# The first output slab is loaded into the weight tiles of the last heads, and the plan's due times for the next slabs and for the new rows' scores are changed

## The chip, the cores and the metric

The kernel runs on one core of a Trainium2 chip. The core has a matrix engine (TensorE, PE in the profile), a vector engine (VectorE, DVE), a scalar engine (ScalarE, ACT), a general engine (GpSimd, POOL) and a queue engine (SyncE, SP). Every engine takes its instructions in order; semaphores join them. 16 transfer engines (DMA) carry data between the memory (HBM) and the core's own memory (SBUF); transfers are issued from SP's and from POOL's queue. TensorE writes its products into eight banks of a small memory (PSUM). The metric is the device time of one execution in microseconds.

## What is computed

The reference is one step of a two-layer decoder for a prompt of 512 rows and for 8 sequences with 4 new rows each (the sample), 1024 wide, with the same weights for both. Layer one has a pooling branch and an attention to 256 memory tokens. Layer two, whose end matters here, has multi-head attention over a shared latent: 8 heads, a latent of 256 and a rotary key of 64. The prompt attends to itself, causally; each sample sequence attends to 4096 cached rows, which lie in 32 pages of 128 rows, and to its own new rows. The heads' results and four memory heads, each times its gate, are 1536 columns; they go through one output projection `w_out` (1536 x 1024), are added to the stream, and a last RMS norm gives `y_prompt` and `y_sample`:

```
mixed = concat([tok * silu(gate_t), mem_o * silu(gate_m)], -1)     # 1536 wide
x = x + mixed @ w_out[l]
y = rmsnorm(x, g_final)
```

All is in 32-bit floats. To be exact on TensorE the prompt's operands are split into a high half (a rounded copy, written by ScalarE) and a low half (the remainder, written by VectorE), and each product is made from three: high x high, high x low, low x high.

## The kernel before

The part that matters is the second layer's attention and its output. There TensorE's order and SP's order are fixed by hand: the program text is their order. The text is written by a small planner, `weave` (line 999). It holds several generators, called threads. Each either yields a condition that must hold before it goes on, or yields the time on TensorE that it has just planned; the plan's clock `now[0]` then moves on by that much. Of the threads that may go on, the one with the smallest `behind()` comes next. Two counters, `act` and `dve`, reckon with the time of ScalarE and VectorE, and `banks` (line 997) notes until when each kind of PSUM bank is held; `tr` has one bank, `ac`, `pa` and `hs` have two each. The plan is a reckoning only: on the chip every instruction waits for its semaphores. ScalarE, VectorE and POOL are not ordered by hand; a scheduler orders them by what it reckons to be ready.

These threads matter. `round_scores` and `round_values` (lines 1069 and 1138) run through the cached pages in 16 rounds of 16 pages, half a round at a time: `turn_keys` transposes the key columns of two pages (`b`) into the bank `tr`, the scores follow; the values take the transposed softmax weights, and once they have read a page buffer, `load_half` puts the next pages' loads on SP's queue (line 1056). `weights_ahead` (line 1261) splits the heads' weights. It runs for the query weights and for four pairs of key and value weights, 8 loads `wu` of 256 KB from POOL's queue into two tiles; each load goes out once the split of two loads before has freed its tile. `scores` and `heads` make the eight prompt heads; a head's `turn_weights` transposes its softmax weights, and its values follow.

When the last head's scores are planned, the pool `heads_in` is closed, and `fin` takes its memory (line 1488): three raw tiles `wr` of 512 KB, three high halves `wh`, three low halves `wl`. The last stage then plans six threads together (line 1669). `own_scores` (line 1638) multiplies the new sample rows' queries with their own keys, 24 products into the bank `tr`, which VectorE reads (line 1652). `first_slabs` (line 1528) loads the first three slabs of `w_out` from POOL's queue and splits them; a slab is 256 rows of `w_out` by 512 columns, the unit in which the output projection runs, and the first three hold heads 0 and 1, 2 and 3, 4 and 5. `mix_b` splits the gated heads themselves. `out_all` runs the output projection of the prompt: first the three slabs for the first 128 rows, then all six for the rest.

Of the kernel before, what the change touches and what calls it, by code (L numbers as in the profile page):

```python
# [8 lines left out]
F32R = mybir.dt.float32r  # L9
# [6 lines left out]
P = 128  # L16
# [22 lines left out]
def trunk_kernel(ctx: ExitStack, tc: tile.TileContext, A, O):  # L39
    nc = tc.nc  # L40
# [35 lines left out]
    def fr(ap):  # L76
        return ap.bitcast(F32)
# [10 lines left out]
    def split(h, l, src, eng=None):  # L88
        nc.scalar.copy(h, src)  # L89
        (eng or nc.vector).tensor_tensor(out=l, in0=src, in1=fr(h), op=ALU.subtract)  # L90
        return h, l
# [51 lines left out]
    for k in range(KD):  # L143
        nc.sync.dma_start(xT[k], A["x_T"][k])
        if k in (0, 3):
            c = slice(k and 4, k + 4 + (k > 0))
# [69 lines left out]
    def load_w(src, k, c):  # L216
        t = pw("wr")
        v = t[:, : k * c].rearrange("p (k c) -> p k c", k=k)
        nc.sync.dma_start(v, src)
        return t, v  # L220

    def split_w(t, k, c, eng=None, pool=None):
        n = k * c
        pool = pool or pw
        h, l = split(pool("wh", F32R, n), pool("wl", F32R, n), t[:, :n], eng)
        return h.rearrange("p (k c) -> p k c", k=k), l.rearrange("p (k c) -> p k c", k=k)
# [293 lines left out]
    for k in range(KD):  # L520
        for i in range(2):
            wh, wl = (t.rearrange("p (k c) -> p k c", k=KD) for t in fw[i])
# [13 lines left out]
    t, v = load_w(wa[22], KD, P)  # L536
    wh, wl = split_w(t, KD, P)
# [133 lines left out]
    order = [8, 9, 10, 11, 6, 7, 4, 5, 2, 3, 0, 1]  # L671
# [3 lines left out]
    for f in range(KD):  # L675
        pts = [ps_("pa"), ps_("pa")]
        for s in range(2):
            t = pw("wr")
            nc.sync.dma_start(t[:, :768], wo[f, s].rearrange("p k c -> p (k c)"))
            wh, wl = split_w(t, 6, P, nc.gpsimd)  # L680
# [32 lines left out]
    for f in (2, 0, 1):  # L713
        c = P if f < 2 else 64
        t, v = load_w(wkv[:, f * P : f * P + c].rearrange("(k p) c -> p k c", p=P), KD, c)
        if f < 2:
            wh, wl = split_w(t, KD, c)
# [28 lines left out]
    for j in range(4):  # L746
        t = xo("o")
# [220 lines left out]
    now = [0.0]  # L968
# [13 lines left out]
    act, dve = Queue(), Queue()  # L982
# [14 lines left out]
    banks = {t: Slots(n) for t, n in (("tr", 1), ("ac", 2), ("pa", 2), ("po", 1), ("hs", 2))}  # L997
# [30 lines left out]
    def ps_(tag):  # L1028
        return (rb if tag in rb.tags else hb)(tag)

    def width(n, full):

        return 0.13 + (full - 0.13) * n / 512

    hq = Pool("hq", "right", qw=(384, 2), tab=(512, 2), wu=(512, 2))
# [209 lines left out]
    total = 122.0  # L1245
# [12 lines left out]
    def pat(tag, dt=F32, n=None):  # L1258
        return next(p for p in (hq, heads_val, heads_in) if tag in p.tags)(tag, dt, n)

    def weights_ahead(raw, load, total, tags, n_cols, at):

        for n in range(total):
            yield lambda: n < 2 or at[n - 2][0] is None
            yield lambda: act.free <= now[0] + 0.2 and dve.free <= now[0] + 0.4
            t = split(pat(tags[0], F32R), pat(tags[1], F32R), raw.pop(n))
            done = dve(act(now[0], width(n_cols, 0.6)), width(n_cols, 0.69))
            at[n] = [t, done]
            if n + 2 < total:
                raw[n + 2] = load(n + 2)  # L1270
            yield 0.0, 5.0 if n else 0.0

    q_at, pair_at = {}, {}

# [150 lines left out]
    def heads():  # L1425
# [49 lines left out]
    rope_x, rope_of, inputs_of, valued_by, es_of = {}, {}, {}, {}, {}  # L1475
    first = [
        Thread(weights_ahead(raw_q, load_q, 12, ("qh", "ql"), 384, q_at), -2.0, 0.0, 1.0, now[0]),
        Thread(weights_ahead(raw_pair, load_pair, 8, ("wuh", "wul"), 512, pair_at), -1.5, 0.0, 1.0, now[0]),
        Thread(ropes(), -1.0, 0.0, 1.0, now[0]),
    ]  # L1480
# [7 lines left out]
    fin = Pool("fin", "left", wr=(D, 3), wh=(D, 3), wl=(D, 3), lo=(512, 1))  # L1488
    mixed = {}

    def load_mix(k):
        if k in (6, 7) or k < 4:
            return gt[k][:, :SEQ]
        t = pat("tab")
        nc.gpsimd.dma_start(t, gmd[k - 8] if k >= 8 else ad[k - 4])
        return t

    def mix_b(k, t=None):
        t = load_mix(k) if t is None else t
        low = fin("lo", F32R) if k == 0 else pg("g", F32R) if k < 4 else pat("p", F32R) if k >= 8 else pt("t", F32R)  # L1500
        mixed[k] = split(pc("c", F32R), low[:, :SEQ], t)
# [2 lines left out]
    ssq = st(16)  # L1504
    sss = st(2)
    slabs = [(fh, s) for fh in range(2) for s in range(6)]
    order = ([0, 1], [2, 3], [4, 5], [8, 9], [10, 11], [6, 7])

    def slab(t, fh, s, queue=None):
        k = order[s][0]  # L1510
        v = t.rearrange("p (k c) -> p k c", k=2)
        src = wo[k * P : (k + 2) * P, fh * 512 : (fh + 1) * 512]
        (queue or nc.sync).dma_start(v, src.rearrange("(k p) c -> p k c", p=P))
        return v

    def prepare(fh, s, t=None):
        if t is None:
            if fh == 0:
                for k in order[s]:
                    mix_b(k)  # L1520
            t = fin("wr")
            slab(t, fh, s)
        wh, wl = split(fin("wh", F32R), fin("wl", F32R), t)
        return wh.rearrange("p (k c) -> p k c", k=2), wl.rearrange("p (k c) -> p k c", k=2)

    prepared, prepared_at = [], []

    def first_slabs():

        raw = [fin("wr") for s in range(3)]  # L1530
        for s, t in enumerate(raw):
            slab(t, *slabs.pop(0), nc.gpsimd)
        at = now[0] + 4.0
        for s in range(3):
            yield lambda: gt[order[s][1]] is not None
            mix = [(k, load_mix(k)) for k in order[s]]
            for k, t in mix:
                yield lambda: act.free <= now[0] + 0.2 and dve.free <= now[0] + 0.4
                mix_b(k, t)
                dve(act(now[0], 0.57), 0.69)  # L1540
            yield lambda: at + 2.0 * s <= now[0] and act.free <= now[0] + 0.2 and dve.free <= now[0] + 0.4
            prepared.append(prepare(0, s, raw[s]))
            prepared_at.append(dve(act(now[0], 1.04), 1.2))

# [17 lines left out]
    def out_rows(fh):  # L1562
# [50 lines left out]
        for s in range(6):  # L1613
            wh, wl = prepared.pop(0)
            late.append((s, wh, wl))
            if s == 4:
                continue
            for j in range(fh == 0 and s < 3, 4):
                for p, piece in enumerate(pieces[j]):
                    for one in late:  # L1620
                        run(one[0], j, piece, *one[1:])
                        yield 1.4 / len(pieces[j]), 0.0
                    if s == 5:
                        if not x1n:
                            yield lambda: x1n
                        done(j, p, *piece)
            for _ in late:
                if slabs:
                    prepared.append(prepare(*slabs.pop(0)))
            late = []  # L1630
# [6 lines left out]

    def own_scores():

        ps = ps_("tr")  # L1640
        sv = ps[:NS, :NS].rearrange("p (b t) -> p b t", b=NB)
        for b in range(NB):
            for k in range(2):
                nc.tensor.matmul(
                    sv[:, b, :], lhsT=QT[:, k, b, :], rhs=ckT_s[:, k, b * NT : (b + 1) * NT], start=k == 0, stop=False
                )
            nc.tensor.matmul(
                sv[:, b, :], lhsT=Qr[:, b, 0, :], rhs=krT_s[:, b * NT : (b + 1) * NT], start=False, stop=True
            )
        w = pat("qw")  # L1650
        tail = w[:NS, :NS].rearrange("p (b t) -> p b t", b=NB)
        nc.vector.tensor_tensor(
            out=tail,
            in0=sv,
            in1=cp[:NS, C_TMASK : C_TMASK + NT].unsqueeze(1).broadcast_to([NS, NB, NT]),
            op=ALU.add,
        )
        tst = w[:NS, 64:80]
        nc.vector.tensor_reduce(out=tst[:, :NB], in_=tail, axis=AX.X, op=ALU.max, negate=True)
        nc.vector.tensor_tensor(out=tail, in0=tail, in1=tst[:, :NB].unsqueeze(2).broadcast_to([NS, NB, NT]), op=ALU.add)  # L1660
        nc.scalar.activation(w[:NS, :NS], w[:NS, :NS], AF.Exp)
        nc.vector.tensor_reduce(out=tst[:, NB:], in_=tail, axis=AX.X, op=ALU.add)
        own.extend([tail, tst])
        yield 0.5, 0.0

    os_ = Thread(own_scores(), 1.0, 0.0, 1.0, now[0])
    fs = Thread(first_slabs(), -1.0, 0.0, 1.0, now[0])
    out = Thread(out_all(), 112 / total, 66 / total, 66.0, now[0])
    weave([fs, rv, rs, ha, os_, out], [fs, ha, os_])
# [294 lines left out]
```

## Time and profile before

| | |
|---|---|
| runs shown | 817.63 us median of 3 (816.04 to 821.03) |
| profiled execution, device time | 821.19 us |
| its span in the profile | 819.3 us |
| TensorE busy | 784.6 us, 96% of the span |
| granted TensorE clock, mean | 0.988 |
| transfers | 169.54 MB, mean 207 GB/s |

The profile names tiles without their numbers; `out<-in` says which tile an instruction writes and which it reads. Times are microseconds from the start of the span. A granted clock of 1.00 is 2.4 GHz, 0.50 is 1.2 GHz. Output products read `wh` and `wl`; the key page that is transposed is `b`; L94, L95, L96, L135, L89 and L90 are lines of helpers (the three products, the transpose, the two halves of a split). L1411 is the mask of a prompt head's scores, and L1417 the last step of its softmax.

### The profile page before, as it was taken

What the parts mean: (1) busy time and instruction counts of PE and PEld (TensorE: products, weight loads), DVE (VectorE), ACT (ScalarE), POOL (GpSimd) and SP (SyncE); (2) the same over time, 40 slices, a digit from 0 to 9 for tenths busy, and PEclk for the clock granted to TensorE, in tenths of its full rate; (3) what the DMA queues carried; (4) which work ended last, traced back from release to release, by engine and by line L of the source; (5) the groups of instructions that cost most, each with busy time, mean ns of one, the idle gap of its engine ahead of it and who ended that gap; (6) DMA issues with size and microseconds to landing.
All of it is one profiled execution on the core that took longest, in us unless ns stands there. A gap on an engine that the chain in (4) does not pass through costs nothing.

```text
span 819.3 us, 17418 instructions
## 1 busy us (share of the span) xinstructions
PE 784.6 (96%) x6834; PEld 670.3 (82%) x6834; DVE 495.3 (60%) x982; ACT 324.6 (40%) x649; POOL 156.9 (19%) x163
## 2 busy tenths in 40 slices
PE   8999999999999999899999999999999999799995
PEld 7989998999999989677989997667767777567674
DVE  7757667698734535765766643666675756634523
ACT  8453334332323225344443322554464545321212
POOL 0035221111234313310532121210000101002001
PEclk9999999999999999989999999999999999899998
DMA  8366247522122326626724889987898988894734
GB/s 304 104 183 228 78 174 264 162 78 66 28 84 90 86 96 216 201 82 214 250 65 145 292 278 372 379 304 271 320 313 282 315 313 302 295 348 145 261 114 176
DMA packets 83251, 169.54 MB, mean 207 GB/s; under 512 B 9441, under 2 KB 26466, under 8 KB 82914
## 3 DMA queue, kind: packets, MB, share of 16 engines
q1 hardware_dynamic: 76930, 148.04, 53.3%
q0 software_dynamic: 6240, 20.39, 6.6%
q8 instruction: 54, 0.88, 0.4%
q14 instruction: 27, 0.22, 0.1%
HBM read 157.19 MB, written 11.21 MB: 206 GB/s over the span
## 4 chain that ended last, share of the span: by engine, by line
PE 82%; DMA 6%; ACT 5%; DVE 4%; issue 1%; SPq 1%; POOL 1%; POOLq 0%; DVEq 0%; ACTq 0%
PE pa L94 17%; PE pa L96 16%; PE pa L95 16%; PE tr L135 4%; PE ac L1156 3%; PE ac L1122 3%; PE hs L94 2%; DMA b<-in_cache_P 2%; PE hs L96 2%; PE hs L95 2%; PE ac L1112 2%; DMA wq<-in_w_q 1%; PE ac L403 1%; PE hs L135 1%; ACT t L1372 1%
## 5 line engine op out<-in xcount | busy, mean ns | idle before, releaser
L94 PE MATMUL pa<-h,wh 128*128 128x272 f32 x832 | 239.9, 291 | 0.0
L96 PE MATMUL pa<-h,wl 128*128 128x272 f32 x832 | 237.3, 290 | 0.2 <-POOL wl L90 0.2
L95 PE MATMUL pa<-h,wh 128*128 128x272 f32 x640 | 184.4, 289 | 0.0
L94 PEld LDWEIGHTS pa<-h,wh 128*128 128x128 f32 x832 | 157.2, 189 | 4.1 <-issue 3.1
L89 ACT CAST wh<-wr 128x1024 fp32r<-128x1024 f32 (+1 forms) x87 | 87.6, 1009 | 183.4 <-PE pa L95 67.6
L96 PEld LDWEIGHTS pa<-h,wl 128*128 128x128 f32 x832 | 155.9, 189 | 2.1 <-issue 1.4
L95 PEld LDWEIGHTS pa<-h,wh 128*128 128x128 f32 x640 | 121.1, 189 | 0.9
L90 POOL TENSOR_TENSOR wl<-wr,wh 128x1024 fp32r<-128x1024 f32 (+1 forms) x41 | 90.5, 2208 | 132.9 <-ACT wh L89 132.8
L90 DVE TENSOR_TENSOR wl<-wr,wh 128x1024 fp32r<-128x1024 f32 x46 | 56.1, 1223 | 34.8 <-ACT wh L89 34.2
L95 PE MATMUL pa<-g,wh 128*128 128x272 f32 x192 | 54.4, 288 | 0.0
L274 ACT ACTIVATE t<-g 128x272 f32<-128x272 f32 x40 | 16.6, 427 | 58.9 <-DVE g L261 58.9
L275 DVE SCALAR_TENSOR_TENSOR g<-t,g 128x272 f32<-128x272 f32 x40 | 32.9, 831 | 6.7 <-ACT t L274 6.7
L1122 PE MATMUL ac<-kt,c 128*32 128x256 f32 x128 | 33.9, 388 | 2.7 <-ACT kt L1086 2.3
L95 PEld LDWEIGHTS pa<-g,wh 128*128 128x128 f32 x192 | 36.1, 188 | 0.0
L1122 PE MATMUL ac<-a,c 128*32 128x256 f32 x384 | 34.3, 388 | 0.0
L261 DVE SCALAR_TENSOR_TENSOR g<-pa,r 128x272 f32<-128x272 f32 x38 | 16.4, 438 | 27.0 <-PE pa L96 26.9
L1156 PE MATMUL ac<-a,rt 128*32 128x256 f32 x384 | 31.4, 383 | 0.2
L1156 PE MATMUL ac<-b,rt 128*32 128x256 f32 x128 | 31.2, 383 | 0.0
L1415 ACT ACTIVATE e<-hs,s 128x128 f32<-128x128 f32 (+3 forms) x32 | 16.9, 529 | 31.0 <-DVE s L1413 30.9
L1156 PEld LDWEIGHTS ac<-a,rt 128*32 128x32 f32 x384 | 14.0, 109 | 14.1 <-issue 2.8
L95 PE MATMUL pa<-wl,mh 128*128 128x512 f32 x64 | 25.0, 402 | 0.4 <-DVE wl L90 0.3
L94 PE MATMUL pa<-wh,mh 128*128 128x512 f32 x64 | 23.4, 401 | 1.6 <-ACT wh L89 1.6
(440 smaller groups left out, 1792.6 us busy)
## 6 DMA issues: line engine op xcount, KB each, us to landing
a<-in_cache_P SPq DMA_DIRECT2D x192, 288.0 KB, 5.7
wr<-in_w_in_a SPq DMA_DIRECT2D x22, 512.0 KB, 3.7
b<-in_cache_P SPq DMA_DIRECT2D x64, 160.0 KB, 6.0
wr<-in_w_in_b SPq DMA_DIRECT2D x19, 512.0 KB, 3.6
cs<-in_mem_kT SPq DMA_DIRECT2D x16, 512.0 KB, 5.8
wr<-in_w_out_a SPq DMA_DIRECT2D x16, 384.0 KB, 3.1
ws<-in_w_out_b SPq DMA_DIRECT2D x12, 512.0 KB, 4.8
wr<-in_w_out_b SPq DMA_DIRECT2D x9, 512.0 KB, 5.8
```

The lines of the kernel that those rows point to most:

```text
L89: nc.scalar.copy(h, src)
L90: (eng or nc.vector).tensor_tensor(out=l, in0=src, in1=fr(h), op=ALU.subtract)
L94: nc.tensor.matmul(out, lhsT=wh, rhs=xh, start=start, stop=False)
L95: nc.tensor.matmul(out, lhsT=wh, rhs=xl, start=False, stop=False)
L96: nc.tensor.matmul(out, lhsT=wl, rhs=xh, start=False, stop=stop)
L135: nc.tensor.transpose(out, in_, ident[:k, :k])
L261: nc.vector.scalar_tensor_tensor(out=out[:, o : o + HALF], in0=ps[:, :HALF], scalar=scale, in1=bc[:, o : o + HALF], op0=ALU.mult, op1=ALU. ...
L274: nc.scalar.activation(th[:, :HALF], z[:, o : o + HALF], AF.Tanh)
L275: nc.vector.scalar_tensor_tensor(out=z[:, o : o + HALF], in0=th[:, :HALF], scalar=1.0, in1=z[:, o : o + HALF], op0=ALU.add, op1=ALU.mult,)
L1122: nc.tensor.matmul(o[j * NS : (j + 1) * NS, :], lhsT=QT[:, k, b, :], rhs=nat[ih][0][:, 2 * j : 2 * j + 2, c] if j < 3 else kt[ih][:, k], s ...
L1156: nc.tensor.matmul(po[j * NS : (j + 1) * NS, :256], lhsT=pT[:, i * P + j * NS : i * P + (j + 1) * NS], rhs=nat[i // 2][j // 3][:, 2 * j % ...
L1415: nc.scalar.activation(e, ps[:, :n], AF.Exp, bias=nx, accum_out=sm)
```

## The change

It has three parts. In `weights_ahead`, where the last two pairs of weights have no successor to load, the freed tiles `wu` now take slab 0: two loads of 128 rows by 512 columns, from POOL's queue. `first_slabs` then loads only slabs 1 and 2, and `prepare` splits slab 0 in two halves of 512 columns. The due times at which the plan lets the three splits happen go from 4, 6 and 8 to 0, 10 and 13 on its clock. `own_scores` now waits in the plan for the bank `tr`, holds it until VectorE has read it, and counts 1.8 instead of 0.5 of TensorE's time.

```diff
@@ weights_ahead
             if n + 2 < total:
                 raw[n + 2] = load(n + 2)
+            elif load is load_pair:
+                t = hq("wu")
+                k = order[0][0] + n + 2 - total
+                nc.gpsimd.dma_start(t, A["w_out_b"][k * P : (k + 1) * P, :512])
+                early.append(t)
             yield 0.0, 5.0 if n else 0.0
@@ prepare
-        wh, wl = split(fin("wh", F32R), fin("wl", F32R), t)
+        wh, wl = fin("wh", F32R), fin("wl", F32R)
+        if t is early:
+            for k in range(2):
+                c = slice(k * 512, k * 512 + 512)
+                split(wh[:, c], wl[:, c], t[k])
+        else:
+            split(wh, wl, t)
@@ first_slabs
-        raw = [fin("wr") for s in range(3)]
+        raw = [early] + [fin("wr") for s in range(2)]
         for s, t in enumerate(raw):
-            slab(t, *slabs.pop(0), nc.gpsimd)
-        at = now[0] + 4.0
+            fh = slabs.pop(0)
+            if s:
+                slab(t, *fh, nc.gpsimd)
+        at = now[0]
...
-            yield lambda: at + 2.0 * s <= now[0] and act.free <= now[0] + 0.2 and dve.free <= now[0] + 0.4
+            yield lambda: at + (0.0, 10.0, 13.0)[s] <= now[0] and act.free <= now[0] + 0.2 and dve.free <= now[0] + 0.4
@@ own_scores
+        yield lambda: banks["tr"].open()
+        slot = banks["tr"].take()
         ps = ps_("tr")
...
-        yield 0.5, 0.0
+        banks["tr"].until[slot] = dve(now[0] + 2.0, 0.2, 0.2, 0.2)
+        yield 1.8, 0.0
```

## Rows read from the trace of the kernel before

**Rows 1.** The page: busy us, share of the span, instructions.
```profile
PE 784.6 (96%) x6834; PEld 670.3 (82%) x6834; DVE 495.3 (60%) x982; ACT 324.6 (40%) x649; POOL 156.9 (19%) x163
```

**Rows 2.** Table by stage: length, busy us by engine, granted clock, DMA share, GB/s.
```profile
690.00:700.00 10.00, 7.74 (x104) 5.66 (x103) 7.97 (x24) 3.61 (x10) 1.67 (x3) 0.90 1.03 381
700.00:710.00 10.00, 7.90 (x56) 4.92 (x56) 5.72 (x15) 5.69 (x12) 0.00 (x0) 0.76 1.01 352
...
730.00:740.00 10.00, 10.00 (x74) 7.60 (x73) 2.45 (x2) 3.44 (x5) 0.00 (x0) 1.00 0.69 250
```

**Rows 3.** The same table in stretches of five us: PE, PEld, DVE, ACT, POOL.
```profile
605.00:610.00 5.00, 3.64 (x17) 2.62 (x15) 3.78 (x11) 3.22 (x9) 0.54 (x1) 1.00 1.02 359
...
640.00:645.00 5.00, 5.00 (x51) 3.30 (x49) 3.56 (x7) 3.46 (x7) 0.57 (x2) 1.00 0.64 242
...
695.00:700.00 5.00, 2.85 (x53) 2.23 (x52) 4.28 (x12) 1.21 (x3) 0.00 (x0) 0.81 1.03 392
700.00:705.00 5.00, 4.96 (x41) 3.01 (x41) 1.70 (x6) 1.77 (x4) 0.00 (x0) 0.51 1.02 353
705.00:710.00 5.00, 2.94 (x16) 1.91 (x16) 4.02 (x10) 3.92 (x9) 0.00 (x0) 1.00 0.99 351
```

**Rows 4.** Timeline of TensorE: start, length, instruction, idle before and its releaser.
```profile
697.52 0.30 PE L135 MATMUL tr<-c,b 128*128 128x128 f32 x1 [0.73 <-DVE qw L1652]
699.24 0.90 PE L135 MATMUL tr<-c,b 128*128 128x128 f32 x3 [1.42 <-DMA b<-in_cache_P]
...
708.39 0.49 PE L94 MATMUL pa<-wh,c 128*128 128x512 f32 x1 [1.30 <-ACT wh L89]
709.65 0.50 PE L95 MATMUL pa<-wl,c 128*128 128x512 f32 x1 [0.77 <-DVE wl L90]
...
713.62 0.63 PE L135 MATMUL tr<-c,b 128*128 128x128 f32 x4
...
732.77 0.60 PE L135 MATMUL tr<-c,b 128*128 128x128 f32 x4
```

**Rows 5.** The chain that ended last: start, length, piece.
```profile
688.68 10.51 DMA b<-in_cache_P
...
711.09 1.93 PE ac L1156 x32
```

**Rows 6.** DMA queues in 688 to 699 (q1 SP, q0 POOL): packets, MB, share.
```profile
q1 hardware_dynamic: 1238, 2.27, 55.2%
q0 software_dynamic: 542, 1.95, 48.2%
```

**Rows 7.** DMA queues in 700 to 705.
```profile
q1 hardware_dynamic: 985, 1.75, 101.1%
q0 software_dynamic: 11, 0.02, 1.4%
```

**Rows 8.** The three slabs issued in 689 to 693, from issue to landing.
```profile
DMA to landing us min/median/max: 7.3/8.7/10.7
```

**Rows 9.** The two key pages issued in 696 to 700, from issue to landing.
```profile
DMA to landing us min/median/max: 6.1/6.7/7.4
```

**Rows 10.** Timeline of POOL: the issue of the three slabs.
```profile
689.54 2.13 POOL L1513 DMA_DIRECT2D wr<-in_w_out_b  x3
```

**Rows 11.** Timeline of SP: the issue of two key pages.
```profile
697.51 2.03 SPq L1056 DMA_DIRECT2D b<-in_cache_P  x2
```

**Rows 12.** Timeline of ScalarE: the last pair's cast, the first slab casts.
```profile
640.06 0.62 ACT L89 CAST wuh<-wu 128x512 fp32r<-128x512 f32 x1 [1.66 <-PE pa L95]
...
707.29 2.94 ACT L89 CAST wh<-wr 128x1024 fp32r<-128x1024 f32 x3
```

**Rows 13.** Timeline of VectorE: the last head's third and fourth mask, its softmax.
```profile
692.42 0.30 DVE L1411 TENSOR_TENSOR hs<-hs,c 128x128 f32<-128x128 f32 x1
...
695.22 0.30 DVE L1411 TENSOR_TENSOR hs<-hs,c 128x128 f32<-128x128 f32 x1
...
698.81 0.47 DVE L1417 TENSOR_SCALAR e<-e,s 128x512 f32<-128x512 f32 x1
```

More of the change, by code (lines that the diff above doesn't have):

```diff
@@ L1270, in weights_ahead @@
                 raw[n + 2] = load(n + 2)
+            elif load is load_pair:
[3 more added lines that the diff above has]
+                early.append(t)
             yield 0.0, 5.0 if n else 0.0
+    early = []
+    order = ([0, 1], [2, 3], [4, 5], [8, 9], [10, 11], [6, 7])
     q_at, pair_at = {}, {}
@@ L1506, in trunk_kernel @@
     slabs = [(fh, s) for fh in range(2) for s in range(6)]
-    order = ([0, 1], [2, 3], [4, 5], [8, 9], [10, 11], [6, 7])
     def slab(t, fh, s, queue=None):
```

## The prediction, made before the change was run

> **What bounds the kernel.** I read the page first: TensorE is busy 96% of the span [rows 1], so time is won only where TensorE waits or runs at its lower clock. The table by stage shows where that is near the change: TensorE works 7.74 and 7.90 us of 10 in 690-700 and 700-710, and is full by 730-740 [rows 2]. The five-us table adds the clock: 0.81 granted in 695-700, 0.51 in 700-705, 1.00 after that [rows 3]. As time at the lower level, 1.2 GHz, that is 0.19 x 5 x 2 + 0.49 x 5 x 2 = 6.8 us; about 1.1 us of it TensorE stood still, so 5.7 us of work ran at half speed, which cost 2.85 us.
>
> TensorE's timeline has four stops there [rows 4]: behind the new rows' scores 0.73 us for the bank (VectorE's read of those scores), 1.42 us for the second key page, and ahead of the first output products 1.30 us for slab 0's high half and 0.77 us for its low half. Together 4.22 us. Why the page is late: the chain has it 10.51 us on the way [rows 5], where the next two took 6.1 and 7.4 us [rows 9]; just behind it POOL issues the three slabs [rows 10]. Why the halves are late: ScalarE begins the three slab casts only at 707.29 [rows 12], and VectorE follows.
>
> **The change part by part.**
>
> *Slab 0 goes out earlier.* One POOL issue of 0.71 us (a third of 2.13) goes, and slabs 1 and 2 issue that much sooner [rows 10]. Two such issues come in, each behind the split that frees its tile: the last pair's high half is cast at 640.06 [rows 12], so the second quarter-MB leaves near 641.5, the first one pair earlier. POOL is busy 0.57 of 5 us there, and the transfer engines have a share of 0.64 [rows 3]: I cost both at nothing. Were that cover gone, each would push a cache page by 0.262 MB / 0.35 MB/us = 0.75 us [rows 7], so 1.5 us at most.
>
> *The late page.* In 688-699 POOL's queue moved 1.95 MB and SP's 2.27 MB, 0.177 and 0.206 MB/us side by side [rows 6]; in 700-705 POOL's moved 0.02 MB and SP's 0.35 MB/us [rows 7]. So POOL's traffic ended near 700. Without 0.524 MB it ends 0.524 / 0.177 = 3.0 us sooner, at 697.1; the 0.43 MB that SP's queue moved from then to 699.2 go in 1.25 us instead of 2.1. The page lands 0.85 us earlier. Bounds: 0, if what goes ahead of it lies wholly before 697.1, and 1.42, the whole wait. I take 0.85, from the two queues' measured rates.
>
> *The halves.* Slab 0 now lies on the chip some 45 us before it is split. Its split is two casts of 0.62 us like the pair's for one of a third of 2.94 [rows 12], and two half-size subtractions on VectorE for one; on ScalarE that is 0.26 us more, beside TensorE's work. The low half's tile lies over memory that the last head's scores read; they end where VectorE's last mask begins, 695.22 [rows 13]. From then VectorE has some 8 us before TensorE wants the half. Both stops, 2.07 us, go; bounds 0 (a stop of the same length elsewhere) and 2.07. Late next would be slabs 1 and 2: they land at most 10.7 us after 691.0, the last third of the issue, so by 701.7 [rows 8, 10], and their products now stand behind more work: no wait.
>
> *The plan.* It issues nothing; it moves TensorE's and SP's order. I followed the loop by the costs written in it, for the order alone. Before, in the last stage: new rows' scores, page transposes, page scores, last head's first two turns and first product, softmax transposes, rest of the turns, slab 0, values of that round, end of the head, next page's transposes, slab 1. Now the bank counts as held for 2.8 us, but no other thread is open then, so the transposes still stand next; behind them the head's two turns, the page scores, slab 0 among the head's products, the next round's first page, and only then the softmax transposes, slab 1 and the values. Hence the 0.73 us stop stays. I take it unchanged; its bounds are a gain of 0.73 and a loss of about 1.3, should slab 0's two low halves stand before that read on VectorE. The turns now come right behind the page transposes and need the last softmax, done at 698.81 + 0.47 [rows 13]; with the clock low the transposes end about there: 0 to 0.4 us, taken as 0.
>
> *The next page.* Its transposes stood at 713.62 [rows 4]. They move up by the 2.9 us won and by what is now behind them: values 1.93 [rows 5] and four softmax transposes, 0.63 like these four [rows 4]. That is 708.2. Their key pages were issued by 699.5 and took 6.1 to 7.4 us, so they lie there by 706 [rows 9, 11]: 2 us to spare. The last pages are issued once the values free their buffers, at about 711 as before, and are used from 732.77 on [rows 4]. TensorE is full there [rows 2], so what is won reaches the end.
>
> **Sum.** -0.85 - 2.07 = -2.9 us. The profiled execution took 821.19, giving 818.3; it lies 3.6 us above the median of the runs shown, 817.63, and the same step from the median gives 814.7.
>
> **Rivals.**
>
> *The clock stays up.* It fell near 698, after the four-column products of the new rows' scores, the stop of 0.73 and the start of the page wait; it did not fall in 605-610 with 1.36 us idle, nor in 705-710 with 2.06 us idle [rows 3]. If the shorter wait keeps it up, 2.85 us more are won: 817.63 - 5.75 = 811.9; the next page is then reached at 705.4, level with its landing. Against: everything up to the page wait is as before, the small products and the first stop included. The Trainium skill, "TensorE: Matmul & The Clock Gate" (Part 1), says that the throttled clock is the default and that activity releases it, and its paragraph on oscillation blames waits for transfers; by that rule the shorter wait wins this rival's 811.9. The two stretches that kept their clock bear the rule out as far as idle time goes, but tell nothing of the small products.
>
> *The waits move.* Slab 0's low halves take about 1.3 us of VectorE just when it carries the bank's read and the last softmax; a first stop of 0.73 + 1.3 and up to 1.2 us before the turns give back 2.5 of the 2.9 us: 817.2. For: VectorE is busy 4.28 of 5 us in 695-700 [rows 3].
>
> *Slower: VectorE is held.* It takes its instructions in order, and the low half cannot start before 695.2. If it is put ahead of the last head's third mask at 692.42 [rows 13], that and all behind it start at 695.2 + 1.3 = 696.5, 4.1 us late; the last softmax ends at 703.4, and TensorE, done with the page transposes near 699.3, stands 4.1 us in place of the 2.9 won: +1.2, or 818.8; up to 820 where the bank's read is late as well. It decides as soon as that subtraction stands ahead of 692.42. Against: VectorE's rows stand in the order in which they came ready.
>
> *It does not do what it says.* POOL's queue could hold the early loads behind a later head's store, but 40 us are to spare and nothing is lost. If instead slab 0's split still stood behind the last head's casts, as at 707.29 [rows 12], only the page's 0.85 is won: 816.8.
>
> **Numbers.** Forecast 0.45 (814.7, its own range 813 to 816.5), clock kept 0.12, waits move or the split stays late 0.26, VectorE held or a like stop 0.17. The predicted time is 814.7. The range goes from 810.5 (clock kept and the whole page wait gone, with 0.8 us for the first stop) to 820 (VectorE held, at its bound). What a measurement of this kernel can tell from no change is about 1%, 8 us: below 809.5 needs the clock kept and every wait at its bound, above 825.8 a stop that no row shows. Faster 0.08, same 0.86, slower 0.06.
>
> **What would show it.** Right: no stop ahead of the first output products; the second key page under 10 us on the way and its wait near 0.6; a granted clock near 0.5 again for some 6 us after the new rows' scores; slab 0's casts before 700. Wrong: a wait of the last head's turns for the softmax, a wait for the next round's key page near 705, or page waits in 640-690.

## The result: 0.31% slower, and the profile after

The changed kernel took 820.26 us (median of 20 executions, 815.93 to 824.49), the kernel before 817.67 us beside it (20 executions). The ratio is 1.0031, with a 95% interval of 1.0016 to 1.0046: 2.6 us slower, where 2.9 us of gain had been forecast, and 0.3 us outside the range. The profiled execution took 822.31 us, its span is 820.5 us and its mean granted clock 0.988.

The page's line of TensorE's busy time (us, share of the span, instructions) answers to [rows 1]; nothing moved there.

```profile
PE 784.5 (96%) x6834; PEld 669.7 (82%) x6834; DVE 495.7 (60%) x983; ACT 324.7 (40%) x650; POOL 156.3 (19%) x164
```

The table by stage (columns as in [rows 2, 3]) shows both signs. TensorE works 0.4 and 0.6 us more in 690-700 and 700-710 than before. But 730-740, full before, now has 2.5 us without work.

```profile
690.00:700.00 10.00, 8.14 (x118) 6.38 (x120) 8.14 (x24) 5.90 (x14) 0.00 (x0) 0.77 1.04 388
700.00:710.00 10.00, 8.54 (x81) 5.69 (x73) 7.30 (x16) 3.89 (x8) 1.07 (x2) 0.89 0.73 253
730.00:740.00 10.00, 7.45 (x46) 4.65 (x45) 2.45 (x2) 1.81 (x3) 0.00 (x0) 0.66 0.43 148
...
695.00:700.00 5.00, 3.46 (x31) 3.07 (x35) 4.17 (x13) 2.12 (x6) 0.00 (x0) 0.53 1.05 385
700.00:705.00 5.00, 5.00 (x36) 3.26 (x29) 2.45 (x9) 2.19 (x5) 0.00 (x0) 0.79 0.81 298
...
730.00:735.00 5.00, 2.45 (x34) 0.97 (x32) 2.45 (x2) 1.81 (x3) 0.00 (x0) 0.79 0.54 191
735.00:740.00 5.00, 5.00 (x17) 3.68 (x13) 0.00 (x0) 0.00 (x0) 0.00 (x0) 0.53 0.33 105
```

In the last five-us rows the granted clock falls a second time, to 0.79 and 0.53, where it was 1.00 before [rows 2]. TensorE's timeline says why there. It answers to [rows 4]: the stops for the page and for slab 0's halves are gone, and slab 0's first product at 701.80 waits for nothing. The stop for the bank has grown from 0.73 to 1.86 us, two others have come (0.37 and 1.28), two small ones of before have gone (0.21 and 0.38), and one of 2.55 us stands where nothing had stood.

```profile
696.54 1.12 PE L135 MATMUL tr<-c,b 128*128 128x128 f32 x4 [1.86 <-DVE qw L1670]
...
701.80 0.65 PE L94 MATMUL pa<-wh,c 128*128 128x512 f32 x1
...
706.20 0.39 PE L102 MATMUL po<-p,vx 128*128 128x256 f32 x1 [0.37 <-DVE p L90]
...
710.18 0.66 PE L135 MATMUL tr<-c,b 128*128 128x128 f32 x4 [1.28 <-DVE rt L1148]
...
728.38 0.60 PE L135 MATMUL tr<-c,b 128*128 128x128 f32 x4
...
733.50 0.63 PE L1122 MATMUL ac<-kt,c 128*32 128x256 f32 x1 [2.55 <-ACT kt L1086]
```

The row at 728.38 is the page transpose that stood at 732.77 [rows 4]. The whole stage starts at another time in each execution, so I count from the new rows' first product: 695.11 before, 693.00 after. The transpose then comes at 35.38 in place of 37.66, 2.3 us sooner: up to here most of the forecast 2.9 us seems to be there (1.42 of it is not the change's doing, as the experiments show). The last output product comes at 115.80 in place of 112.56, 3.2 us later. Between the two lie 5.5 us of loss: the stop of 2.55 us, and the second fall of the clock, 6.8 us at 1.2 GHz by the two rows above. Some 6 us of that were work at half speed, which cost about 3 us.

The stop is a matter of ScalarE. Its timeline, before and after, between 729 and 735 (start, length, instruction, idle before and what ended it); `wh<-wr` are the casts of slabs 3 and 4, `kt<-tr` copies the transposed page out of PSUM for the scores:

```profile
729.81 1.05 ACT L89 CAST wh<-wr 128x1024 fp32r<-128x1024 f32 x1 [5.41 <-DMA wr<-in_w_out_b]
...
733.01 1.05 ACT L89 CAST wh<-wr 128x1024 fp32r<-128x1024 f32 x1 [1.88 <-PE po L96]
733.96 0.58 ACT L1086 COPY kt<-tr 128x512 f32<-128x512 f32 x1
```

```profile
729.23 1.05 ACT L89 CAST wh<-wr 128x1024 fp32r<-128x1024 f32 x1 [4.61 <-DMA wr<-in_w_out_b]
731.91 1.04 ACT L89 CAST wh<-wr 128x1024 fp32r<-128x1024 f32 x1 [1.64 <-DMA wr<-in_w_out_b]
732.86 0.58 ACT L1086 COPY kt<-tr 128x512 f32<-128x512 f32 x1
```

The order is the same: cast, cast, copy. Before, the second cast waited for TensorE, and the copy came 0.6 us after the page was transposed (732.77 + 0.60). After, TensorE has the page ready at 728.98, but ScalarE stands in front of slab 4's transfer until 731.91, and the copy waits in line behind: 3.9 us late. The chain of work that ended last runs through a cache page, the slab's transfer behind it and the copy (start, length, piece):

```profile
718.16 5.07 DMA a<-in_cache_P
723.30 8.51 DMA wr<-in_w_out_b
...
732.86 0.59 ACT kt L1086
```

And why are the slabs no earlier, if TensorE is? They stand behind the last key pages on SP, and those wait for the values of that round to free their buffers. SP issued the last pages at 711.88 and the slabs behind them from 722.52; before it was 712.13 and 723.88. What TensorE won did not move the transfers with it. Counted from the new rows' first product, the slabs left at 28.8 us before and at 29.5 after: the plan's new order has put that round's values later, at 17.8 us against 15.9.

### The profile page after: what moved, and what is told of

Its sections match the earlier page's. It is cut to its first block, busy times and chain, and to the rows that moved or that the text cites. A ratio compares the mean times of both kernels' runs of the same rounds, so it can differ in the third digit from the quotient of the medians.

```text
span 820.5 us, 17423 instructions
## 1 busy us (share of the span) xinstructions
PE 784.5 (96%) x6834; PEld 669.7 (82%) x6834; DVE 495.7 (60%) x983; ACT 324.7 (40%) x650; POOL 156.3 (19%) x164
## 4 chain that ended last, share of the span: by engine, by line
PE 75%; DMA 8%; DVE 6%; ACT 5%; issue 2%; SPq 1%; POOL 1%; POOLq 0%; DVEq 0%; ACTq 0%
PE pa L94 16%; PE pa L96 15%; PE pa L95 15%; PE tr L135 4%; PE ac L1122 3%; PE ac L1156 3%; PE hs L94 2%; DMA b<-in_cache_P 2%; PE ac L1112 2%; PE hs L95 1%; PE hs L96 1%; DMA x<-x1d 1%; PE ac L403 1%; PE hs L135 1%; DMA wr<-in_w_out_b 1%
```

## The experiments

Each kernel was run 5 to 12 times beside the kernel before (817.4 to 817.9 us in each set), and one execution of each was traced. A ratio is to the kernel before, with its 95% interval. Theory S: the key copy waits in line on ScalarE behind a cast whose transfer is late. Rival D: the early transfer itself costs (its memory traffic, its smaller splits). Rival P: the plan's new figures cost by the order that they give to TensorE.

**The early transfer alone.** The change with the due times and the scores' step of before:

```diff
-            yield lambda: at + (0.0, 10.0, 13.0)[s] <= now[0] ...
+            yield lambda: at + (4.0, 6.0, 8.0)[s] <= now[0] ...
...
-        banks["tr"].until[slot] = dve(now[0] + 2.0, 0.2, 0.2, 0.2)
-        yield 1.8, 0.0
+        yield 0.5, 0.0
```

> Slab 0 early, the plan as before: TensorE's order is the old one. Theory S (what slab 0 wins is lost again where ScalarE, taking its casts in order, stands at slab 4's cast until that slab has landed, with the copy of the last round's first keys queued behind; TensorE waits 2.55 us for the copy there and runs 6.8 us at 1.2 GHz after it): the two stops for slab 0's halves go, the bank's stop grows to 1.9, TensorE comes to the last round's keys about 1.5 to 2 us early, so the wait for the copy is 0 to 1 us and the clock does not fall there: -1 to -2 us against the kernel before. Rival D (the early transfer itself and VectorE's two subtractions slow the heads): +2 us, as the whole change.

Measured 816.21 us, ratio 0.9991 (0.9974 to 1.0009). Rival D is refuted: by itself the transfer costs nothing that the runs show, and wins perhaps 1 us (the interval holds no gain as well). TensorE's order is that of before; the values come sooner, at 13.4 us, SP issues the slabs 26.0 us after the new rows' first product, against 29.5 us in the change, and no stop on the key copy is seen.

**The plan's two edits, each without the rest.** The due times alone (4, 10, 13, with nothing loaded early), and the scores' step alone:

> Only the due times: 4, 10 and 13 instead of 4, 6 and 8. TensorE's order differs in one place, slab 1 stands behind the next page's scores instead of ahead of them. Theory S: nothing is won early, so nothing is lost at the last round: within 0.5 us of the kernel before. Rival P (the later slabs in the plan are what costs): +2 us.

> Only the new rows' scores with their length and bank in the plan. TensorE's order becomes nearly that of the change up to the head's end, and the last rounds move too: the first keys of the last round stand ahead of the slab casts on ScalarE. Theory S: the stops for slab 0's halves stay in part, no wait for the copy at the last round: 0 to -2 us. Rival P (the new order of the plan costs): +2 us.

The due times alone: 818.25 us, ratio 0.9999 (0.9985 to 1.0014), nothing. The scores' step alone: 819.70 us, ratio 1.0017 (1.0004 to 1.0031), a loss of about 1.4 to 1.8 us. Its stops between the new rows' scores and 50 us after them add up to 5.56 us against 4.81 before; the largest is 1.69 us, the values waiting for a copy on VectorE. Rival P holds for this one edit.

The two kernels also tell something of the late page. In both POOL still issues all three slabs, yet neither waits for the page. TensorE and POOL with the due times alone, and the way of the two key pages in question:

```profile
694.95 0.66 PE L135 MATMUL tr<-c,b 128*128 128x128 f32 x4 [0.66 <-DVE qw L1652]
...
687.04 2.13 POOL L1513 DMA_DIRECT2D wr<-in_w_out_b  x3
...
DMA to landing us min/median/max: 5.1/5.3/5.5
```

With the scores' step alone those pages took 4.8 and 5.5 us. In the trace of the kernel before they took 10.1 and 10.5; that execution (821.19 us) was slower than all 20 that were run beside the change (814.8 to 821.0). As far as single traces tell, the wait of 1.42 us belonged to that execution and not to the three slabs; why its pages were late stays open.

**The early transfer with one edit of the plan.**

> The early transfer and the new length of the scores' step, with the old due times. The plan then puts the key copy of the last round ahead of the casts of slabs 3 and 4 on ScalarE. Theory S (the copy waits in line behind casts whose transfers are late): no stop on the key copy of 2 us and no second fall of the clock; the time is the early transfer's 816.2 plus the 1.5 us or so that the scores' length cost alone, about 817 to 818. Rival P (the new length of the scores' step itself costs the change its time, whatever the copy waits for): 820, as the change.

> The early transfer and the new due times, with the old length of the scores' step. The plan puts the values of that round before the last turned probabilities, so the last pages and slabs 3 and 4 are asked for as early as before or earlier; the order on ScalarE at the last round is that of the change (cast, cast, key copy). Theory S: slabs 3 and 4 are not late, no stop above 1 us on the key copy, one fall of the clock, about 816 us. Rival P' (due times together with the early transfer cost): 819 to 820, with the stop on the key copy there.

With the scores' step: 817.68 us, ratio 0.9996 (0.9981 to 1.0011). With the due times: 816.43 us, ratio 0.9978 (0.9965 to 0.9990). Neither of these pairs makes the 820.3 us. The third pair, due times and scores' step with nothing loaded early, was not run; the scores' step alone, at 819.70 us, is not clearly apart from the change. The first of the two tells most. ScalarE's timeline there:

```profile
726.77 0.59 ACT L1086 COPY kt<-tr 128x512 f32<-128x512 f32 x1 [3.27 <-PE tr L135]
728.71 1.05 ACT L89 CAST wh<-wr 128x1024 fp32r<-128x1024 f32 x1 [1.35 <-DMA wr<-in_w_out_b]
730.03 1.04 ACT L89 CAST wh<-wr 128x1024 fp32r<-128x1024 f32 x1 [0.26 <-DMA wr<-in_w_out_b]
```

The page is transposed 3.6 us after the slabs were issued (5.9 us in the change), and both casts wait for transfers. But the copy stands ahead of them, and TensorE has no stop for it. That a transfer is late costs nothing by itself; what stands behind its cast decides.

**The late slabs from another queue.** The change, with slabs 3 and 4 issued from POOL's queue, which has no pages in it:

```diff
-            slab(t, fh, s)
+            slab(t, fh, s, nc.gpsimd if fh == 0 and s in (3, 4) else None)
```

> The change, with the loads of slabs 3 and 4 (first half of the columns) issued from POOL's queue, where nothing holds them, instead of from SP's behind the last cache pages. They land some 10 us earlier. Theory S: no wait for the key copy at the last round and no second fall of the clock, so 2.55 + 2.9 = 5.4 us less than the change, less up to 1 us for a third slab beside the late key page: 815 to 816.5 us against 820.3. Rivals D and P: no slab cast is what costs, so 820 as with the change.

Measured 818.28 us, ratio 1.0001 (0.9987 to 1.0016): 2.0 us under the change, not the 3.8 to 5.3 expected. The stop of 2.55 us and the second fall are gone, but a stop of 0.91 us has come at 719.83, and the one of 1.28 us became 1.50.

**The order on ScalarE alone.** The change, with the casts of slabs 3 and 4 put behind the key copy; all transfers and the orders on TensorE, SP and VectorE stay:

```diff
+        if fh == 0 and s == 3:
+            held.append((wh, wl, t))
+        elif fh == 0 and s == 4:
+            with tc.issue_after(key[-1]):
+                split(wh, wl, t)
...
-                    nc.scalar.copy(x, ps)
+                    key.append(nc.scalar.copy(x, ps).ins)
+                    while held:
+                        with tc.issue_after(key[-1]):
+                            split(*held.pop())
```

> The change with one thing altered: ScalarE takes the key copy of the last round ahead of the casts of slabs 3 and 4 (in the change it comes behind both). TensorE's order, SP's order, all transfers and VectorE's order stay. Theory S (the copy waits in line behind a cast whose transfer is late): the stop of 2.55 us on the key copy goes, the granted clock stays up after 720 us of the span, and the time falls by 3 to 4 us in executions that had both, to about 817.5 median against the change's 820.3. Rival (the transfers themselves are late and TensorE waits for slab 3 or 4 instead): the stop comes back as one on wh or wl of 1 to 2.5 us at the first products of slab 3, and the time stays at 819.5 to 820.5.

Measured 816.61 us, ratio 0.9991 (0.9979 to 1.0004): 3.65 us under the change, and no longer slower than the kernel before (0.8 us under it, with 1 inside the interval). ScalarE's timeline, and the five-us table where the stop and the second fall had been:

```profile
728.68 0.58 ACT L1087 COPY kt<-tr 128x512 f32<-128x512 f32 x1 [4.45 <-PE tr L135]
729.16 1.05 ACT L89 CAST wh<-wr 128x1024 fp32r<-128x1024 f32 x1
731.09 1.05 ACT L89 CAST wh<-wr 128x1024 fp32r<-128x1024 f32 x1 [0.88 <-DMA wr<-in_w_out_b]
```

```profile
725.00:730.00 5.00, 5.00 (x28) 3.82 (x30) 0.00 (x0) 1.32 (x2) 0.00 (x0) 1.00 1.02 385
730.00:735.00 5.00, 5.00 (x50) 3.79 (x51) 2.45 (x2) 1.82 (x3) 0.00 (x0) 1.00 0.44 128
735.00:740.00 5.00, 5.00 (x48) 3.51 (x47) 2.84 (x8) 1.85 (x5) 0.00 (x0) 1.00 0.67 209
```

Slab 4's cast still waits for its transfer until 731.09, and nothing waits for it. TensorE is full and its clock at 1.00. Theory S is shown, and the rival of this run, that the stop would come back on slab 3 or 4, is refuted. The first fall of the clock is shorter too in this execution, so its trace cannot say how much of the 3.65 us is the stop and the second fall alone.

**Slab 0's low halves, moved off VectorE's front.** The early transfer alone, with the two halves on POOL; and instead held on VectorE until the read of the scores' bank:

```diff
-                split(wh[:, c], wl[:, c], t[k])
+                split(wh[:, c], wl[:, c], t[k], nc.gpsimd)
```

```diff
-                split(wh[:, c], wl[:, c], t[k])
+                with tc.issue_after(read[0]):
+                    split(wh[:, c], wl[:, c], t[k])
```

> Kernel before plus the early transfer alone (as early_only, 816.2 us), and slab 0's two low halves on POOL in place of VectorE, so that VectorE meets the read of the scores' bank two instructions sooner. If those low halves are what grew the bank stop: the stop on VectorE ahead of the next page goes from 1.86 us back to 0.66 to 0.73, POOL's two halves (half of a 2.41 us row each) end about 3 us after slab 0's high halves, before its first products, and the time is about 815.1 us (ratio near 0.997). If the stop has another cause it stays at 1.9 and the time at 816.2. Rival: POOL's low halves come too late and TensorE stops on wl; then 817 or more.

> The early transfer alone (816.2 us), with slab 0's two low halves held on VectorE until the bank of the new rows' scores is read. If they are what grew that stop from 0.73 to 1.86 us: it goes back to 0.66 to 0.73, and 816.2 less 1.2 is 815.0 us, near the kernel with those halves on POOL (814.2), without the VectorE operations that took 1.16 and 1.64 us there beside POOL's. Rival: the halves now stand ahead of the last softmax's scale on VectorE and the stop moves to the turned probabilities; then 816.

On POOL: 814.19 us, ratio 0.9953 (0.9940 to 0.9967). Held on VectorE: 812.86 us, ratio 0.9949 (0.9923 to 0.9974), the lowest median of all, though the two intervals overlap; of 817.67 us the ratio is 4.2 us. VectorE's timeline in the change, and TensorE's stop and VectorE's timeline with the halves held:

```profile
694.51 0.68 DVE L90 TENSOR_TENSOR wl<-wu,wh 128x512 fp32r<-128x512 f32 x1
695.11 0.69 DVE L90 TENSOR_TENSOR g<-g,c 128x512 fp32r<-128x512 f32 x1
695.71 0.69 DVE L90 TENSOR_TENSOR wl<-wu,wh 128x512 fp32r<-128x512 f32 x1
696.31 0.17 DVE L1670 TENSOR_TENSOR qw<-tr,c 32x32 f32<-32x32 f32 x1
```

```profile
695.78 0.74 PE L135 MATMUL tr<-c,b 128*128 128x128 f32 x4 [0.66 <-DVE qw L1669]
```

```profile
694.95 0.68 DVE L90 TENSOR_TENSOR g<-g,c 128x512 fp32r<-128x512 f32 x1
695.55 0.17 DVE L1669 TENSOR_TENSOR qw<-tr,c 32x32 f32<-32x32 f32 x1
695.65 1.27 DVE L90 TENSOR_TENSOR wl<-wu,wh 128x512 fp32r<-128x512 f32 x2
```

Two halves of 0.6 us stood ahead of the read; behind it they are still early enough for slab 0. The stop went from 1.86 to 0.66 us, the expected 1.2; the median fell by 3.3 us against the early transfer alone, more than that. In the profiled executions the lower clock is shorter as well (below); how much of the 3.3 us that is in the other executions the runs do not settle.

**Both mends in the change itself.**

> The change, with slabs 3 and 4 asked for by POOL's queue in place of SP's (as after_pool34, 818.3 us), and slab 0's two low halves on POOL. If the low halves are what holds VectorE: the bank stop goes from 1.86 to about 0.7 us, 818.3 less 1.2 is 817.1. If the rest of the change's loss is in the stops behind (values waiting for a copy that is queued on VectorE, 1.3 to 1.5 us), those stay, and the kernel does not get under the early transfer alone (816.2).

> The change with both alterations: the key copy ahead of the casts of slabs 3 and 4 on ScalarE, and slab 0's low halves behind the read of the scores' bank on VectorE. The bank stop goes from 1.86 to 0.7 us, but in the change's order the turned probabilities follow at once, and they wait for a scale that now stands behind the two halves on VectorE: about 1.1 us of stop there. So no more than 0.3 us under the kernel with the first alteration alone, about 817.3; if the two gains add, 816.3.

Slabs 3 and 4 from POOL's queue and the low halves on POOL: 819.47 us, ratio 1.0027 (1.0014 to 1.0040). The key copy ahead and the halves held: 818.51 us, ratio 1.0015 (0.9999 to 1.0031). Both misses: expected were 817.1 and about 817.3, and both are slower than with the first mend alone (818.28 and 816.61). In the change's order the turned probabilities come right behind the page and need the last softmax, which now stands behind the halves or beside POOL's. TensorE's stops in the second of the two:

```profile
693.46 1.12 PE L135 MATMUL tr<-c,b 128*128 128x128 f32 x4 [1.10 <-DVE qw L1680]
...
696.52 1.11 PE L135 MATMUL hs<-c,e 128*128 128x128 f32 x4 [1.30 <-DVE e L1430]
...
705.88 0.39 PE L102 MATMUL po<-p,vx 128*128 128x256 f32 x1 [1.25 <-DVE p L90]
```

The bank's stop went to 1.10 us only, not to the 0.7 expected, and the 0.76 us won there came back as 1.30 us one step later, where 1.1 had been expected. The 1.25 us at 705.88 was not expected: VectorE runs two low halves of 1.22 us each, slabs 1 and 2, ahead of a piece of the probabilities.

All profiled executions side by side. Stops: TensorE's idle time in the 50 us from the new rows' scores (before, 1.42 us of it is the page). Clock: mean granted in 690-745. Length: from the new rows' first product to the last output product.

| kernel | median us | stops us | clock | length us |
|---|---|---|---|---|
| before | 817.67 | 4.81 | 0.94 | 112.56 |
| the change | 820.26 | 6.06 | 0.88 | 115.80 |
| early transfer alone | 816.21 | 2.56 | 0.94 | 109.45 |
| due times alone | 818.25 | 3.44 | 0.97 | 110.52 |
| scores' step alone | 819.70 | 5.56 | 0.94 | 112.41 |
| early + scores' step | 817.68 | 3.27 | 0.97 | 108.91 |
| early + due times | 816.43 | 3.50 | 0.97 | 109.47 |
| change, slabs from POOL | 818.28 | 4.43 | 0.94 | 111.63 |
| change, copy ahead | 816.61 | 3.52 | 0.97 | 109.33 |
| early, halves on POOL | 814.19 | 1.70 | 0.97 | 107.66 |
| early, halves held | 812.86 | 1.22 | 0.97 | 107.18 |
| change, slabs and halves on POOL | 819.47 | 5.06 | 0.94 | 112.46 |
| change, copy ahead, halves held | 818.51 | 4.82 | 0.91 | 113.47 |

A length is that of one execution, and the granted clock differs between executions: in the change from 0.984 to 0.994 over the span, and its executions at 0.993 or more took 815.9 to 818.6 us, all others 818.3 to 824.5. So rows are compared by their stops first, and even these do not rank the medians: the due times alone have 3.44 us of stops and 818.25 us, the early transfer with them 3.50 and 816.43.

## Why the prediction was wrong

**The step that failed** stands under "the next page": "TensorE is full there [rows 2], so what is won reaches the end". It looked at the pages, which were indeed issued at about 711 as before (711.88) and came in time. It did not look at what is queued behind them on SP, slabs 3 and 4, nor at ScalarE, where the key copy stands behind the casts of these slabs. Those transfers follow the values, which the plan's new order had put 1.9 us later; with the early transfer alone the slabs went out 2.8 us sooner than before, and nothing waited for the copy. In the change TensorE, 2.3 us ahead, stood 2.55 us for the copy, and its clock fell. Putting the copy ahead of the casts took 3.65 us off the median (3.4 when each kernel is counted against the kernel before beside it): that is more than the whole loss of 2.6 us. The slack could have been read from the kernel before: the copy came 0.6 us after its page there, right behind a cast. The Trainium skill, "TensorE: Matmul & The Clock Gate" (the paragraph on engine queue depths in Part 1), says that ScalarE and VectorE are strictly first in, first out; the copy's 3.9 us behind a cast that waits for its transfer agree.

**The second term** was the bank's stop, taken as unchanged at 0.73 us with a loss of about 1.3 as its bound. It measured 1.86, so the bound was the value: the two low halves did stand ahead of the read. The rival "the waits move" had named this very place. Its second half, a wait of the turns for the softmax, is not in the change, but is in both kernels that kept the change's order and took the halves away from the front (1.07 and 1.30 us).

**Not priced** was VectorE's queue at 709: the copy of the softmax transposes (`rt`) stands behind slab 2's low half, the next heads' splits and a step of their gate. It began 0.5 us after its transposes were done, and the page's transposes, which use the same bank, waited 1.28 us, 0.69 of it for the copy itself. The prediction said of slabs 1 and 2 that they would be late next and cause no wait. Their products did not wait; what stood behind their low halves did. That the low half caused it is read from the order of the rows; no run moved it alone. The plan's part was put at nothing as a whole, and the scores' step by itself cost 1.4 to 1.8 us.

**What was right, and what was luck.** Both stops on slab 0, 2.07 us, are gone, as forecast. The page's wait, 1.42 us, is gone altogether, where 0.85 had been taken; but it is also gone in the two kernels that load nothing early, so this term was no gain of the change, and the reason given for it, POOL's traffic, is not borne out. The first fall of the clock stayed: 0.53 and 0.79 against 0.81 and 0.51 [rows 3], 6.8 us at 1.2 GHz in both. The third mask was not held, so the slower case came by another road than the rival on record. No page waited in 640-690, and POOL's early issues took 0.54 us each. Of the signs on record those for being right came (the page's wait went further than said) and those for being wrong did not: they watched the stage as far as the next page, and the larger loss lies behind it.

The books of the profiled executions: stops gone 3.49 us and 0.59 of small ones; stops grown or new 1.13 + 0.37 + 1.28 + 2.55 = 5.33. That is 1.25 us more of idle time, and the second fall cost about 3 us more. The stage grew by 3.2 us, so about 1 us of gain elsewhere is not accounted for. With the copy ahead the stops are 3.52 us, against 4.81 before, of which 1.42 were the page.

## What to carry to other kernels

- When work is moved forward on the bounding engine, follow not only the transfers it meets next but every helper instruction that stands behind a wait for those transfers on an in-order engine. A wait that costs nothing today is a stop once the consumer comes sooner.
- A wait that stands in one trace need not be in the next. Here a third of the forecast (0.85 of 2.9 us) was the end of such a wait.
- Put what the bounding engine needs next (copies out of PSUM, reads that free a bank) ahead of work that only has to be done some time later. Here the kernels with such a swap, one on ScalarE and one on VectorE, came out 3.65 and 3.3 us lower, the earlier transfer alone about 1 us.
- A mend that works in one order of the work need not add up with another: in the change's own order the same two halves, held back, cost 1.9 us.

## What the runs showed of the hardware

VectorE and POOL slow each other. With slab 0's halves on POOL, VectorE's timeline and POOL's in the same stretch:

```profile
696.18 0.69 DVE L1422 TENSOR_REDUCE s<-hs 128x1 f32<-128x512 f32 x1
696.78 1.16 DVE L90 TENSOR_TENSOR g<-g,c 128x512 fp32r<-128x512 f32 x1
...
697.98 1.64 DVE L90 TENSOR_TENSOR g<-g,c 128x512 fp32r<-128x512 f32 x1
...
699.71 0.66 DVE L90 TENSOR_TENSOR g<-g,c 128x512 fp32r<-128x512 f32 x1
```

```profile
695.62 3.44 POOL L90 TENSOR_TENSOR wl<-wu,wh 128x512 fp32r<-128x512 f32 x2 [4.51 <-ACT wh L89]
```

The same subtraction took 1.16 and 1.64 us beside POOL's and 0.66 us once POOL was done. The second of them ended at 699.62, 0.56 us after POOL's last, about as if it had only then begun; and POOL took 3.44 us for the two halves, where a whole 128x1024 takes it 2.41 us in the kernel before. The reduction ahead of them, which has one input, in PSUM, ran beside POOL's first half and kept its 0.69 us (0.68 in the change, at 693.91). The Trainium skill, "SBUF — State Buffer" ("Who interferes with whom"), says that a VectorE instruction with two inputs in SBUF contends with a GpSimd instruction that reads SBUF, and that one with at most one input there does not; the two rows agree, and so does the reduction. The longer subtraction stands ahead of the bank's read, and the halves on POOL left 1.14 us of the bank's stop, the halves held on VectorE 0.66.

The clock also fell where TensorE hardly stood still: with the halves held no transfer is waited for, the one stop near it is 0.66 us, and 695-700 has 0.66 granted, the next row 1.00.

```profile
695.00:700.00 5.00, 4.34 (x46) 2.51 (x44) 4.45 (x13) 1.59 (x4) 0.00 (x0) 0.66 1.05 385
700.00:705.00 5.00, 4.65 (x31) 3.17 (x33) 3.77 (x14) 3.85 (x9) 0.00 (x0) 1.00 1.04 374
```

So the rule that the prediction took from the Trainium skill's page on the clock gate, by which the shorter wait would keep the clock up, does not decide here: the fall stayed with the waits for transfers gone, and was only shorter, 0.34 x 5 x 2 = 3.4 us at 1.2 GHz in place of 6.8. It does not come of the new rows' four-column products alone either: with the due times alone they stand there too, behind them a stop of the same 0.66 us, and the clock held until after 700; it fell shortly before 705, after the 1.30 and 0.76 us for slab 0 (0.94 and 0.72).

```profile
695.00:700.00 5.00, 4.50 (x49) 2.74 (x50) 3.98 (x13) 2.57 (x8) 0.00 (x0) 1.00 1.05 384
700.00:705.00 5.00, 2.94 (x15) 2.13 (x13) 4.37 (x10) 3.48 (x5) 0.00 (x0) 0.94 1.06 387
705.00:710.00 5.00, 5.00 (x50) 2.52 (x53) 2.23 (x4) 0.04 (x1) 0.48 (x1) 0.72 0.48 155
```

What lets this first fall come or stay away stays open. The second fall of the change followed the stop of 2.55 us, and is gone in the kernel that took only that stop away.
